# Attention in two layers: the exponentials of a unit issued one unit later than its scores and maxima

## The chip, the cores and the metric

The kernel runs on one core of a Trainium2 chip. Its time is the device time of one execution in microseconds (us). A core has TensorE (PE) for matrix products, VectorE (DVE), ScalarE (ACT) and GpSimd (POOL) for the rest, and SyncE (SP), which here only issues loads. Each engine takes its instructions in the order in which the program gives them. Matrix products write to PSUM, eight banks of 128 x 512 float32, and ACT and DVE read them from there.

## The reference, cut to what matters

Two layers over 256 latent and 256 context tokens. Each layer normalizes, projects, runs a pooling mixer and a differential attention side by side, projects out, and ends with a mixture of 32 experts. The attention, which the change concerns, is for each of four heads

```python
def diff_attend(q, k, v, lam):
    s = jnp.einsum('bqhmd,bkhmd->bhmqk', q, k).astype(jnp.float32) * (ATTN_HEAD_DIM ** -0.5)
    p = jax.nn.softmax(s, axis=-1)          # m = 0, 1: two maps a head
    a = p[:, :, 0] - lam * p[:, :, 1]
    return jnp.einsum('bhqk,bkhe->bqhe', a.astype(v.dtype), v)
```

Context queries see the 256 context keys, latent queries all 512 keys. In the second layer only latent queries are left.

## The kernel before, in words

A layer is `mixer`, which ends with the output projection, and `Moe`, which streams the experts' weights from memory. In `mixer` the attention works in *units*: one block of 128 queries and one head. Layer 0 has 16 units (the first 8 are context queries with 256 keys, the last 8 latent ones with 512), layer 1 has 8, all with 512 keys. A unit goes through four functions:

- `scores(i)`: PE makes two score tiles `S` (L712), DVE takes each row's maximum (L714) and scales it to the negative bias `nb` (L717), and ACT makes two exponentials `e` out of `S` with the row sums (L720). With that the two PSUM buffers of `S` come free.
- `probs(i)`: DVE turns the sums into a factor (L729, L730) and combines the two maps into one tile (L731).
- `turned(i)`: PE turns that tile (L739) into the PSUM tile `aT`, and ACT copies it to `t` (L741).
- `values(i)`: PE multiplies `t` with the values (L753) into `o`, and ACT squares the result for the norm (L755).

The code that stands around them sets each engine's order, word for word. `scores` of units 0, 1, 2 and `probs(0)` come first, mixed with pieces of the pooling mixer (`pool_a`: tile `pl`, copied at L686; `pool_b`: tile `pm`, copied at L694 and split at L463) and with broadcasts `bc` copied at L456. Then the loop runs over the units: `turned(i)`, `probs(i + 1)`, `scores(i + 3)`, `values(i)`, and other work behind it: pieces of the modulation (`ada`, L414), products of the output projection (`wo`, L467 to L469, twelve matrix products each), and the splitting of its weights `wout` into a high part `wh` (ACT) and a low part `wl` (DVE and POOL), both at L463 and L464, in runs of four pieces.

All PSUM tiles but one come from seven buffers, handed out in the order in which they came free. `e` has five buffers; from unit 2 to unit 6 of layer 0 two of them hold a bias of the modulation.

Of the kernel before, what the change touches and what calls it, by code (L numbers as in the profile page):

```python
# [231 lines left out]
def backbone_kernel(ctx: ExitStack, tc: tile.TileContext, x, par_d, lam_d, modb_d, adaw, win, wout, wx, rw_d, pw_d, fg_d,  # L232
# [16 lines left out]
    def w2(tag, dt=F32, shape=None):  # L249
        uid[0] += 1  # L250
        return work.tile(shape or [128, 512], dt, tag=tag, bufs=BUFS[tag], name=f"{tag}{uid[0]}")

    def small(shape, dt=F32, tag="sm", bufs=4):
        uid[0] += 1
        return work.tile(shape, dt, tag=tag, bufs=bufs, name=f"{tag}{uid[0]}")
# [10 lines left out]
    def pump():  # L266
        while pending and len(SB.slots) - pending[0][1] >= keep[pending[0][0][0] == "xf"] and (pending[0][0][0] != "xf" or early[0] > 0):
            key, n, fn = pending.popleft()
            early[0] -= key[0] == "xf"
            loaded[key] = fn()  # L270
# [17 lines left out]
    def fill(us):  # L288

        while us > 0.3 and fillers:  # L290
            key, t, fn = fillers[0]
            if key not in loaded:
                return
            fillers.popleft()
            fn()
            us -= t
# [256 lines left out]
    def mixer(l, W3, rows, pre, late=None):  # L553
# [122 lines left out]
        def pool_a(g):  # L676
            p = PS.get([128, 512], F32, "pl")

            for s in ((1,) if last else (0, 1)):
                for kt, cs in ((0, slice(0, 128)), (1, slice(112, 128)), (1, slice(128, 256)), (0, slice(128, 144))):  # L680
                    o = 256 * s
                    pe.matmul(p.t[:, o + cs.start:o + cs.stop], lhsT=u.t[:, 2 * s + kt, g * 128:g * 128 + 128],
                              rhs=band.t[:, (2 * g + kt) * 256 + cs.start:(2 * g + kt) * 256 + cs.stop],
                              start=kt == cs.start // 128, stop=kt != cs.start // 128)
            pT[g] = w2("m")
            act.activation(pT[g][:, c0:], p.t[:, c0:], AF.Copy)  # L686
            p.free()

        def pool_b(g):
            p = PS.get([128, 512], F32, "pm")  # L690
            pe.matmul(p.t[:, c0:], lhsT=pw[:, g], rhs=pT[g][:, c0:], start=True, stop=True)
            ps_ = par[:, P_PS + 4 * l + g:P_PS + 1 + 4 * l + g]
            m = w2("m")
            act.activation(m[:, c0:], p.t[:, c0:], AF.Copy, scale=ps_)  # L694
            p.free()
            split(m[:, c0:], cP[0][:, g], cP[1][:, g], gp)
# [3 lines left out]
        st, opsum, sums, sq, scaled = {}, {}, {}, {}, {}  # L700

        def scores(i):
            qt, h = units[i]
            nk = 512 if qt >= 2 else 256
            if h == 0:
                sums[qt] = small([128, 4, 2], tag="ls", bufs=3)
            mx, l_ = small([128, 2], tag="mx"), sums[qt][:, h]
            S, e = [], []
            for m in range(2):
                p = PS.get([128, 512], F32, "S")  # L710
                ms = slice(64 * m, 64 * m + 64)
                pe.matmul(p.t[:, :nk], lhsT=qT.t[ms, h, qt * 128:qt * 128 + 128], rhs=kT.t[ms, h, :nk],  # L712
                          start=True, stop=True)
                dve.reduce_max(mx[:, m:m + 1], p.t[:, :nk], axis=AX.X)  # L714
                S.append(p)
            nb = small([128, 2], tag="nb")
            dve.tensor_scalar(nb, mx, -0.125, None, op0=OP.mult)  # L717
            for m in range(2):
                e.append(w2("e"))
                act.activation(e[m][:, :nk], S[m].t[:, :nk], AF.Exp, scale=0.125, bias=nb[:, m:m + 1],  # L720
                               accum_out=l_[:, m:m + 1])
                S[m].free()
            st[i] = (e, l_, nk)

        def probs(i):

            e, l_, nk = st[i]
            r = small([128, 1], tag="rl")
            dve.reciprocal(r, l_[:, 1:2])  # L729
            stt(r, r, lamn[:, l:l + 1], l_[:, 0:1], op0=OP.mult, op1=OP.mult)  # L730
            stt(e[0][:, :nk], e[1][:, :nk], r, e[0][:, :nk], op0=OP.mult, op1=OP.add)  # L731
            st[i] = (e[0], nk)

        def turned(i):
            a, nk = st[i]
            n = nk // 128
            p = PS.get([128, 4, 128], F32, "aT")
            for kt in range(n):
                pe.transpose(p.t[:, kt], a[:, kt * 128:kt * 128 + 128], ident)  # L739
            aT = w2("t").rearrange("p (a b) -> p a b", a=4)  # L740
            act.activation(aT[:, :n], p.t[:, :n], AF.Copy)  # L741
            p.free()
            st[i] = (aT, n)
# [61 lines left out]
        def split_w(nb, kh):  # L805

            def part(k):
                if k == 0:
                    raw = need((key, nb, kh))
                    W[nb, kh] = SB.get([128, 4, 512], F32R, "wh"), SB.get([128, 4, 512], F32R, "wl"), raw  # L810
                hi, lo, raw = W[nb, kh]
                split(raw.t[:, k], hi.t[:, k], lo.t[:, k], dve if k % 2 else gp)
                if k == 0:
                    reserve()
                if k == 3:
                    W[nb, kh] = hi, lo
                    raw.free()
            return [(0.65, lambda k=k: part(k)) for k in range(4)]
# [34 lines left out]
        def pool_part():  # L853
            for nb in range(2):
                if nb and not (last and len(SPLITS) > 0):
                    steps.extend(split_w(1, 0))
                for t in qtiles:
                    steps.append((2.6, lambda t=t, nb=nb: out_unit(t, nb, 0)))
                steps.append((0, lambda nb=nb: release(W.pop((nb, 0)))))
            steps.append((0, lambda: release(pooled)))  # L860
            if not (last and len(SPLITS) > 1):
                steps.extend(split_w(0, 1))
            steps.append((0, lambda: moe or start_moe()))
            if not (last and len(SPLITS) > 2):
                steps.extend(split_w(1, 1))

        def release(hs):
            for h in hs:
                h.free()
# [70 lines left out]
        def start_moe():  # L940
            nonlocal moe
            rw = w2("o")[:, :320].rearrange("p (k n) -> p k n", k=8)
            act.dma_start(rw, rw_d[l].rearrange("p (k n) -> p k n", k=8))
            moe = Moe(l, qtiles, g1 if last else SB.get([128, 2, D], F32, "g2"), rw)
            moe.modulations()
            keep[1] = left[0]

        def spare():

            if moe and any(f[0][0] == "ada" and f[0] in loaded for f in fillers):  # L950
                fill_any()
            elif fillers and (fillers[0][0][0] == "bc" or len(fillers) > RES):
                fill(0.9)

        N = len(units)
        keep[:] = 0, 99
        scores(0)
        pool_a(0)
        for _, fn in split_w(0, 0):
            fn()  # L960
        fill(0.9)
        scores(1)
        pool_a(1)
        pool_b(0)
        fill(0.9)
        probs(0)
        scores(2)
        pool_a(2)
        pool_b(1)
        fill(0.9)  # L970
        for i in range(N):
            turned(i)
            if i + 1 < N:
                probs(i + 1)
            if i + 3 < N:
                scores(i + 3)
            if i == 0:
                pool_a(3)
                pool_b(2)
            if i == 1:  # L980
                pool_b(3)
                release((u, band))
                pool_part()
            if i == MOE_AT[l]:
                start_moe()
            if last and i in SPLITS:
                for _, fn in split_w(*((1, 0), (0, 1), (1, 1))[SPLITS.index(i)]):
                    fn()
            spare()
            values(i)  # L990
            while later and later[0][0] <= i:
                later.popleft()[1]()
            clock[0] += 3.0
            if i == N - EARLY_AT[l]:
                early[0] = EARLY[l]
                pump()
            if i > 1:
                proceed(STEP[l])
# [825 lines left out]
    for cb, k in order:  # L1824
        queue_ada(1, cb, [k])
    want_experts(0)
    moe = mixer(0, [], (ring, {}), pre)

    def next_loads():
# [33 lines left out]

    late = moe.run(next_loads, tail, at_end)
    moe = mixer(1, W3, (rs.pop(), dict(enumerate(rs))), {}, late)

    def finish():
# [51 lines left out]
```

## Time and profile before

| what | us |
|---|---|
| three runs | 961.01, 964.27, 965.11; median 964.27 |
| the profiled execution: its own time | 960.57 |
| its span, first to last instruction | 958.8 |
| PE busy | 814.8 (85%) |
| DVE busy | 441.7 (46%) |
| ACT busy | 265.8 (28%) |
| POOL busy | 174.1 (18%) |
| mean granted TensorE clock | 0.937 of full speed |
| memory read and written | 346 GB/s over the span |

The attention of layer 0 runs from about 148 to 256 us of the span, that of layer 1 from about 678 to 720 us. The shares are averages over stages with different limits: in the expert stages PE and the loads are busy nearly all the time, while in the attention four engines hand work to each other. So the trace is read by stage: which engine stands idle in the attention, and what ends that.

### The profile page before, as it was taken

What the parts mean: (1) busy time and instruction counts of PE and PEld (TensorE: products, weight loads), DVE (VectorE), ACT (ScalarE), POOL (GpSimd) and SP (SyncE); (2) the same over time, 40 slices, a digit from 0 to 9 for tenths busy, and PEclk for the clock granted to TensorE, in tenths of its full rate; (3) what the DMA queues carried; (4) which work ended last, traced back from release to release, by engine and by line L of the source; (5) the groups of instructions that cost most, each with busy time, mean ns of one, the idle gap of its engine ahead of it and who ended that gap; (6) DMA issues with size and microseconds to landing.
All of it is one profiled execution on the core that took longest, in us unless ns stands there. A gap on an engine that the chain in (4) does not pass through costs nothing.

```text
span 958.8 us, 13409 instructions
## 1 busy us (share of the span) xinstructions
PE 814.8 (85%) x4841; PEld 442.2 (46%) x4841; DVE 441.7 (46%) x965; ACT 265.8 (28%) x593; POOL 174.1 (18%) x192
## 2 busy tenths in 40 slices
PE   4799999988995879899976876899879679999973
PEld 1467765545784333333321224687557533443311
DVE  0533414566566222322211846654665735766633
ACT  1532216345441111111100015532572311111101
POOL 1400002233612101111101000000135211222212
PEclk9699999999997899999988997999999689999997
DMA  9989388830628999999999994672237589999992
GB/s 374 417 336 351 133 311 317 337 122 8 246 106 320 376 395 407 418 417 419 417 419 417 382 393 198 224 282 88 99 131 271 220 344 417 418 419 414 419 401 77
DMA packets 49081, 293.80 MB, mean 306 GB/s; under 512 B 7480, under 2 KB 7864, under 8 KB 16752
## 3 DMA queue, kind: packets, MB, share of 16 engines
q1 hardware_dynamic: 37008, 266.78, 69.3%
q0 software_dynamic: 6192, 13.84, 3.7%
q10 hardware_dynamic: 5808, 12.25, 3.4%
q8 instruction: 41, 0.67, 0.3%
q14 instruction: 32, 0.26, 0.1%
HBM read 317.29 MB, written 14.78 MB: 346 GB/s over the span
## 4 chain that ended last, share of the span: by engine, by line
PE 27%; DMA 26%; DVE 7%; ACT 2%; issue 1%; POOL 1%; SPq 0%; POOLq 0%; DVEq 0%; ACTq 0%
DMA we<-in_wx_dram 23%; PE gu L1447 8%; PE dn L1482 5%; DMA ada<-in_adaw_dram 2%; PE pj L599 2%; PE pj L467 2%; PE pj L468 2%; PE pj L469 2%; DMA h<-hd,ix 1%; DVE m L1514 1%; DVE o L1230 1%; PE rowps L414 1%; PE hTp L1268 1%; DVE X L1516 1%; PE hTp L1266 1%
## 5 line engine op out<-in xcount | busy, mean ns | idle before, releaser
L1482 PE MATMUL dn<-we,t 128*32 128x512 f32 (+2 forms) x672 | 108.2, 639 | 6.7 <-DMA we<-in_wx_dram 5.0
L1453 DVE SCALAR_TENSOR_TENSOR t<-t,tb,gu 128x256 f32<-128x256 f32 x25 | 12.0, 481 | 174.1 <-ACT t L1452 174.1
L1447 PE MATMUL gu<-we,hT0modl 128*32 128x512 f32 (+1 forms) x400 | 66.0, 631 | 10.8 <-DMA we<-in_wx_dram 10.1
L1452 ACT ACTIVATE t<-gu 128x256 f32<-128x256 f32 x25 | 9.6, 385 | 224.0 <-PE gu L1447 224.0
L1447 PE MATMUL gu<-we,hT0modh 128*32 128x512 f32 (+1 forms) x400 | 63.6, 628 | 7.1 <-DMA we<-in_wx_dram 6.3
L414 PE MATMUL rowps<-ada,sT 128*32 128x512 f32 x384 | 54.7, 658 | 13.7 <-DMA ada<-in_adaw_dram 13.7
L1482 PEld LDWEIGHTS dn<-we,t 128*32 128x32 f32 (+2 forms) x672 | 29.8, 121 | 66.8 <-issue 53.6
L467 PE MATMUL pj<-hH,wh 128*128 128x512 f32 (+1 forms) x128 | 47.6, 372 | 0.0
L1447 PE MATMUL gu<-we,hT1modl 128*32 128x512 f32 (+1 forms) x272 | 42.6, 604 | 5.5 <-DMA we<-in_wx_dram 5.5
L1516 POOL TENSOR_TENSOR X<-X,m 128x512 f32<-128x512 f32 x20 | 25.6, 1278 | 117.5 <-DVE m L1514 117.3
L469 PE MATMUL pj<-hH,wl 128*128 128x512 f32 (+1 forms) x128 | 46.4, 363 | 0.0
L468 PE MATMUL pj<-hL,wh 128*128 128x512 f32 (+1 forms) x128 | 46.4, 363 | 0.0
L1516 DVE TENSOR_TENSOR X<-X,m 128x512 f32<-128x512 f32 x36 | 43.5, 1208 | 1.3
L1447 PEld LDWEIGHTS gu<-we,hT0modl 128*32 128x32 f32 (+1 forms) x400 | 17.8, 121 | 54.7 <-issue 36.5
L1447 PE MATMUL gu<-we,hT1modh 128*32 128x512 f32 (+1 forms) x272 | 40.4, 625 | 2.5 <-DMA we<-in_wx_dram 1.4
L720 ACT ACTIVATE e<-S,nb 128x512 f32<-128x512 f32 (+1 forms) x48 | 29.2, 613 | 46.7 <-DVE nb L717 31.5
L1447 PEld LDWEIGHTS gu<-we,hT0modh 128*32 128x32 f32 (+1 forms) x400 | 16.9, 120 | 49.4 <-issue 36.5
L714 DVE TENSOR_REDUCE mx<-S 128x1 f32<-128x512 f32 (+1 forms) x48 | 26.8, 596 | 27.6 <-PE S L712 27.4
L1514 DVE TENSOR_TENSOR m<-cb,g 128x512 f32<-128x512 f32 x56 | 36.7, 682 | 0.1
L1249 POOL DMA_INDIRECT h<-hd,ix x14 | 14.4, 1027 | 123.3 <-DVE iy L1256 50.1
L753 PE MATMUL o<-v,t 128*128 128x128 f32 x160 | 24.5, 293 | 10.1 <-ACT t L741 10.1
L753 PEld LDWEIGHTS o<-v,t 128*128 128x128 f32 x160 | 20.1, 194 | 26.2 <-ACT t L741 23.6
(347 smaller groups left out, 1582.0 us busy)
## 6 DMA issues: line engine op xcount, KB each, us to landing
we<-in_wx_dram SPq DMA_DIRECT2D x207, 1024.0 KB
ada<-in_adaw_dram SPq DMA_DIRECT2D x48, 1024.0 KB
YD<-m ACTq DMA_DIRECT2D x1, 4096.0 KB
yb<-YD POOLq DMA_DIRECT2D x4, 1024.0 KB, 22.5
X<-in_x_dram SPq DMA_DIRECT2D x4, 512.0 KB
e<-in_modb_dram ACTq DMA_DIRECT2D x8, 256.0 KB
band<-in_band_dram SPq DMA_DIRECT2D x2, 1024.0 KB
hd<-h ACTq DMA_DIRECT2D x4, 512.0 KB
```

The costliest lines, as they stand in the source:

```text
L414: pe.matmul(rowps[l][32 * j:32 * j + 32], lhsT=sT[:, k, 4 - 2 * cb:36 - 2 * cb], rhs=h.t[:, 512 * j:512 * j + 512], start=cb < 2 and k == ...
L467: pe.matmul(ps, lhsT=lh, rhs=rh, start=first, stop=False)
L468: pe.matmul(ps, lhsT=lh, rhs=rl, start=False, stop=False)
L469: pe.matmul(ps, lhsT=ll, rhs=rh, start=False, stop=last)
L599: pe.matmul(p.t, lhsT=H[kh].t[:, k, ts], rhs=W3[kh][part].t[:, k], start=n == 0, stop=n == 23)
L714: dve.reduce_max(mx[:, m:m + 1], p.t[:, :nk], axis=AX.X)
L720: act.activation(e[m][:, :nk], S[m].t[:, :nk], AF.Exp, scale=0.125, bias=nb[:, m:m + 1], accum_out=l_[:, m:m + 1])
L753: pe.matmul(o.t[:, h], lhsT=aT[:, kt], rhs=v.t[:, kt, h * 128:h * 128 + 128], start=kt == 0, stop=kt == n - 1)
L1447: pe.matmul(p.t[r], lhsT=hT[k // 4][:, k % 4, r], rhs=gate_up(weights(w, k // 4), k), start=k == 0, stop=k == 7)
L1482: pe.matmul(ps[n2].t[r], lhsT=aT[:, k, r], rhs=down_w(weights(w, 2), k, n2), start=k == 0, stop=k == 1)
L1514: tt(m, q, self.g2[stream(t)][:, ns], op=OP.mult)
L1516: e.tensor_tensor(X[:, t, ns], X[:, t, ns], m, op=OP.add)
```

## The change

`scores` loses its last part, the two exponentials, which become a function `exps`. What `exps` needs, the two score tiles and `nb`, is kept until then. In the loop `exps(i + 2)` stands right behind `turned(i)`, ahead of `probs(i + 1)` and `scores(i + 3)`: the exponentials of a unit are given to ACT one pass of the loop after its scores. No instruction is added or removed on any engine, and nothing changes on POOL and SP but line numbers. Lines from L720 on move by 5, from the start of the loop by up to 9.

```diff
             mx, l_ = small([128, 2], tag="mx"), sums[qt][:, h]
-            S, e = [], []
+            S = []
             for m in range(2):
...
             dve.tensor_scalar(nb, mx, -0.125, None, op0=OP.mult)
+            st[i] = (S, nb, l_, nk)
+
+        def exps(i):
+            S, nb, l_, nk = st[i]
+            e = []
             for m in range(2):
                 e.append(w2("e"))
                 act.activation(e[m][:, :nk], S[m].t[:, :nk], AF.Exp, scale=0.125, bias=nb[:, m:m + 1],
...
         scores(1)
+        exps(0)
         pool_a(1)
         pool_b(0)
         fill(0.9)
+        scores(2)
+        exps(1)
         probs(0)
-        scores(2)
         pool_a(2)
         pool_b(1)
         fill(0.9)
         for i in range(N):
             turned(i)
+            if i + 2 < N:
+                exps(i + 2)
             if i + 1 < N:
                 probs(i + 1)
             if i + 3 < N:
```

On ACT in layer 0, from the copy of unit 11 on, the order before is as follows; `S_93` and `S_94` are the scores of unit 14, `aT_92` and `aT_95` the turned tiles of units 11 and 12, `wh` one of the weight splits.

```order
L741 ACTIVATE t153_1698<-aT_92_1693 128x512
L720 ACTIVATE e157_1713,ls136_1600<-S_93_1705,nb156_1711 128x512
L720 ACTIVATE e158_1715,ls136_1600<-S_94_1708,nb156_1711 128x512
L755 ACTIVATE t159_1721,rn130_1559<-o_81_1558 128x128
L463 ACTIVATE wh_87_1723<-('wout', 0)_75_1169 128x512 x4
L741 ACTIVATE t160_1738<-aT_95_1733 128x512
```

And now, at the same place, with `S_88` and `S_89`, the scores of unit 13:

```order
L746 ACTIVATE t151_1694<-aT_92_1689 128x512
L725 ACTIVATE e152_1696,ls136_1600<-S_88_1650,nb147_1656 128x512
L725 ACTIVATE e153_1698,ls136_1600<-S_89_1653,nb147_1656 128x512
L760 ACTIVATE t157_1717,rn128_1555<-o_81_1554 128x128
L463 ACTIVATE wh_87_1719<-('wout', 0)_75_1165 128x512 x4
L746 ACTIVATE t158_1734<-aT_95_1729 128x512
```

Between the two copies the kinds of instructions are the same, but the exponentials are those of the unit whose scores and maxima were issued one pass earlier.

On ACT at the start of layer 1's attention, before (`modh1` ends the modulation, `S_307` and `S_308` are unit 0, `S_312` and `S_313` unit 1):

```order
L436 ACTIVATE modh1_5529<-e392_5160 128x512
L720 ACT_TABLE_LOAD
L720 ACTIVATE e402_5551,ls399_5541<-S_307_5543,nb401_5549 128x512
L720 ACTIVATE e403_5553,ls399_5541<-S_308_5546,nb401_5549 128x512
L686 ACTIVATE m404_5560<-pl_309_5555 128x256
L463 ACTIVATE wh_183_5562<-('wout', 1)_166_5237 128x512 x4
L456 ACTIVATE g1_182_5540<-bc_310_5572 128x512
L456 ACTIVATE g1_182_5540<-bc_311_5576 128x512
L720 ACTIVATE e407_5589,ls399_5541<-S_312_5581,nb406_5587 128x512
L720 ACTIVATE e408_5591,ls399_5541<-S_313_5584,nb406_5587 128x512
L686 ACTIVATE m409_5598<-pl_314_5593 128x256
```

And now:

```order
L436 ACTIVATE modh1_5529<-e392_5160 128x512
L686 ACTIVATE m402_5556<-pl_309_5551 128x256
L463 ACTIVATE wh_183_5558<-('wout', 1)_166_5237 128x512 x4
L456 ACTIVATE g1_182_5540<-bc_310_5568 128x512
L456 ACTIVATE g1_182_5540<-bc_311_5572 128x512
L725 ACT_TABLE_LOAD
L725 ACTIVATE e405_5585,ls399_5541<-S_307_5543,nb401_5549 128x512
L725 ACTIVATE e406_5587,ls399_5541<-S_308_5546,nb401_5549 128x512
L686 ACTIVATE m407_5594<-pl_314_5589 128x256
```

The pool copy, the split and the two broadcast copies have moved ahead of unit 0's exponentials, and the table load has gone with the exponentials; the copy of unit 1's `pl` no longer stands behind unit 1's exponentials.

On ACT near the end of layer 1's attention, before: the copy of unit 5 (`aT_340`) and the last split that stands among the units.

```order
L755 ACTIVATE t458_5808,rn457_5803<-o_339_5802 128x128
L741 ACTIVATE t460_5822<-aT_340_5817 128x512
L463 ACTIVATE wh_185_5828<-('wout', 1)_173_5384 128x512 x4
L755 ACTIVATE t462_5842,rn457_5803<-o_339_5802 128x128
L741 ACTIVATE t464_5851<-aT_341_5846 128x512
```

And now:

```order
L760 ACTIVATE t456_5804,rn455_5799<-o_339_5798 128x128
L746 ACTIVATE t458_5818<-aT_340_5813 128x512
L725 ACTIVATE e459_5820,ls430_5692<-S_337_5790,nb454_5796 128x512
L725 ACTIVATE e460_5822,ls430_5692<-S_338_5793,nb454_5796 128x512
L463 ACTIVATE wh_185_5828<-('wout', 1)_173_5384 128x512 x4
L760 ACTIVATE t462_5842,rn455_5799<-o_339_5798 128x128
L746 ACTIVATE t464_5851<-aT_341_5846 128x512
```

The exponentials of the last unit, unit 7, now stand between that copy and the split.

## Rows read from the trace of the kernel before

**Rows 1.** The chain that ended last, in order of time: start, us, what.

```profile
406.95 20.57 DMA we<-in_wx_dram
...
697.67 1.28 DVE mx L714 x2
699.18 1.45 ACT e L720 x4
701.70 0.50 ACT t L741
702.24 1.16 PE o L753 x8
...
842.38 18.62 DMA we<-in_wx_dram
```

**Rows 2.** Waits from 146 to 250 us: total us, times, longest.

```profile
ACT e L720 <- DVE nb L717: 23.3, 11, 4.6
...
PE o L753 <- ACT t L741: 6.3, 4, 3.3
```

**Rows 3.** Timeline of PE, layer 0: start, us, what, [idle before <-releaser].

```profile
143.48 2.76 PE L414 MATMUL rowps<-ada,sT 128*32 128x512 f32 x24
...
193.54 1.79 PE L712 MATMUL S<-kT,qT 64*128 64x512 f32 x4 [0.33 <-ACT e L720]
...
203.32 0.71 PE L753 MATMUL o<-v,t 128*128 128x128 f32 x4 [1.42 <-ACT t L741]
...
207.49 2.35 PE L712 MATMUL S<-kT,qT 64*128 64x512 f32 x4
...
232.55 1.66 PE L753 MATMUL o<-v,t 128*128 128x128 f32 x8 [3.29 <-ACT t L741]
234.14 3.90 PE L414 MATMUL rowps<-ada,sT 128*32 128x512 f32 x24
...
240.90 1.16 PE L753 MATMUL o<-v,t 128*128 128x128 f32 x8 [1.27 <-ACT t L741]
```

**Rows 4.** Timeline of ACT, layer 0, units 11 to 13.

```profile
225.65 0.60 ACT L741 ACTIVATE t<-aT 128x512 f32<-128x512 f32 x1 [0.25 <-PE aT L739]
228.23 0.69 ACT L720 ACTIVATE e<-S,nb 128x512 f32<-128x512 f32 x1 [1.98 <-DVE nb L717]
...
229.82 2.19 ACT L463 ACTIVATE wh<-('wout', 0)_75_1169 128x512 fp32r<-128x512 f32 x4
...
236.58 0.69 ACT L720 ACTIVATE e<-S,nb 128x512 f32<-128x512 f32 x1 [4.08 <-DVE nb L717]
```

**Rows 5.** Timeline of PE, layer 1.

```profile
689.93 0.77 PE L691 MATMUL pm<-m,o 128*128 128x256 f32 x2 [2.57 <-ACT m L686]
690.49 1.06 PE L739 MATMUL aT<-cst,e 128*128 128x128 f32 x4
...
703.76 1.13 PE L712 MATMUL S<-kT,qT 64*128 64x512 f32 x4
...
706.44 1.13 PE L712 MATMUL S<-kT,qT 64*128 64x512 f32 x4
...
709.69 0.60 PE L739 MATMUL aT<-cst,e 128*128 128x128 f32 x4
```

**Rows 6.** Timeline of ACT, layer 1.

```profile
678.68 1.28 ACT L720 ACT_TABLE_LOAD   x1
...
682.51 2.19 ACT L463 ACTIVATE wh<-('wout', 1)_166_5237 128x512 fp32r<-128x512 f32 x4
...
711.20 2.20 ACT L463 ACTIVATE wh<-('wout', 1)_173_5384 128x512 fp32r<-128x512 f32 x4
```

**Rows 7.** Timeline of DVE, layer 1.

```profile
683.70 3.02 DVE L464 TENSOR_TENSOR wl<-('wout', 1)_166_5237,wh 128x512 fp32r<-128x512 f32 x2 [2.83 <-ACT wh L463]
```

**Rows 8.** Stretches of layer 0: length, busy us by engine, granted clock, DMA share, GB/s.

```profile
196.00:206.00 10.00, 6.95 (x42) 3.95 (x39) 5.59 (x10) 5.32 (x13) 4.65 (x3) 1.00 0.56 211
...
226.00:236.00 10.00, 6.71 (x40) 3.57 (x40) 6.38 (x10) 4.51 (x12) 4.92 (x4) 0.85 0.00 0
```

## The prediction

> **What bounds the kernel now.** I read the page's shares first, then the chain that ended last, then the waits and each engine's timeline within the two attention stretches. In the chain the long steps are loads of expert weights, 20.57 us from 406.95 and 18.62 us from 842.38 [rows 1]: the expert stages are held by the stream of weights. The attention is not: in 226 to 236 us the loads stand still (share 0.00), while PE is busy 6.71 us of 10, DVE 3.57, ACT 6.38 and POOL 4.51 [rows 8]. No engine is full there, so the time lies in waits for one another. In layer 1 the chain shows the ring that they form: maxima on DVE (L714, 1.28 for two), exponentials on ACT (L720, 1.45 for a pair), copy `t` on ACT (0.50), values on PE (L753, 1.16) [rows 1].
>
> The waits tell which link is late. ACT waits for `nb` in front of the exponentials 23.3 us in 11 waits, and PE waits for ACT's copy `t` 6.3 us in 4 [rows 2]. The two are one thing seen twice. ACT takes its instructions in order, and the exponentials of a unit stand ahead of the copy of an earlier unit. While ACT stands at exponentials whose maxima PE and DVE are only making, it can't copy, and PE stands at the values. Idle time of ACT alone would cost nothing; what counts is the 6.3 us on PE and PE's waits for score buffers.
>
> **Layer 0, buffers (A).** The scores at 193.54 wait 0.33 us and then take 1.79 instead of 1.13, those at 207.49 take 2.35 instead of 1.13 [rows 3, 5]: 0.33 + 0.66 + 1.22 = 2.2 us, in which the group stops for a buffer that earlier exponentials hold. With the exponentials a pass later these buffers are held longer, but all seven go round, so which release a score tile needs changes too. Following the rotation in the new order, I find scores that wait for a copy of the same pass (0.60, [rows 4], half of it hidden), twice, and once for a DVE step of about the same length: estimate 1.0 us. Net gain 1.2; bounds 0 and 2.2.
>
> **Layer 0, the copy of unit 12 (B).** Before the values at 232.55 PE is idle 3.29 us, released by `t` [rows 3]. On ACT the copy of unit 11 is over at 226.25, the next exponentials wait 1.98 us for `nb` until 228.23, and behind them come a square, four weight splits (2.19 us) and then the copy PE wants [rows 4]. Now the exponentials there have had their `nb` for a pass, so the 1.98 goes. The square still needs unit 11's values, and the splits still stand ahead of the copy. I take 1.7: the 1.98 less about half of a copy's 0.60. Bounds: 1.0 (half the wait, if the square comes late) and all 3.29.
>
> **Layer 0, the next copy (C).** Exponentials wait 4.08 us for `nb` until 236.58 [rows 4], and the values at 240.90 have 1.27 us of idle ahead [rows 3]. Without that wait the copy is done while PE runs 24 modulation products (3.90 us, [rows 3]): the 1.3 goes whole, covered by these products. Without that cover at most the same 1.3 would stay.
>
> **Layer 0, the clock (D).** Behind the idle 3.29 the values at 232.55 take 1.66 us against 1.16 at 240.90, and 24 products at 234.14 take 3.90 against 2.76 at 143.48 [rows 3]; the granted clock of this stretch is 0.85, a mix of the upper level with the lower [rows 8]. That is 0.50 + 1.14 = 1.6 us. After B the idle ahead of it is about 1.6. The nearest row is the idle of 1.42 at 203.32, in a stretch that kept a clock of 1.00 [rows 3, 8], so I take the whole 1.6; bounds 0 and 1.6. The 1.42 itself stays: there ACT is busy with splits and copies, not waiting at exponentials.
>
> Layer 0: 1.2 + 1.7 + 1.3 + 1.6 = 5.8 us.
>
> **Layer 1, the start (E).** Unit 0 is turned at 690.49, behind a `pm` product that waited 2.57 us for the copy of `pl`, which stood behind unit 1's exponentials [rows 5]. Two moves act here. The pool copy, the split and the broadcasts go ahead of unit 0's exponentials, and with them go 1.28 of table load and two exponentials of 0.69 [rows 6, 4], 2.66 together; since the copy of `pl` waits for its own product, the split comes about 2.1 earlier than 682.51 [rows 6]. DVE's two `wl` (3.02 us, having waited 2.83 for the split [rows 7]) come that much earlier, and then the maxima of units 1 and 2 (1.28 for two, [rows 1]). The exponentials of unit 0, and the table load directly before them, now lie on the path to `probs(0)`. The turn comes at about 688.5: gain 2.0. Bounds 0.7 (the load's 1.28 counts once more) and 2.6 (all of the wait).
>
> The Trainium skill, "ScalarE: Activation LUTs", section "What ACT_TABLE_LOAD costs", puts a drain of 1380 ns behind the 1283 ns of a load. The trace has the 1.28 [rows 6], and no row here shows a drain apart from it. By the page the gain of E would be 1.4 smaller, and the time 1.4 longer; the sum goes without it.
>
> **Layer 1, the loop (F).** From the turn of unit 0 at 690.49 to that of unit 5 at 709.69 it is 19.2 us, 3.84 a unit, while near its end two units' scores stand 706.44 - 703.76 = 2.68 apart [rows 5]. At 2.68 five units are 13.4 us; three pool pieces like the `pm` of 0.77 [rows 5] make it 15.7, a gain of 3.5. Each unit has four maxima and `probs` on DVE and a pair of exponentials on ACT, which keep some of it; I take 3.0. Bounds: 1.5 (a pair of exponentials, 1.45 [rows 1], leaves the ring once) and 19.2 - 13.4 = 5.8.
>
> **Layer 1, the end (G).** The exponentials of unit 7 now stand ahead of the last four splits at 711.20 [rows 6] and of the copies behind them: a loss of 1.45 at most [rows 1], which I take; the other bound is 0.
>
> Layer 1: 2.0 + 3.0 - 1.45 = 3.6. The rest of the change (the list `e`, the tuple that is kept) makes no instruction, and POOL and SP are moved past nothing.
>
> **What becomes of the gain.** The loads stand still in the attention [rows 8] because their buffers are full, and they start again when the expert stage takes the buffers. So a shorter attention starts that stream earlier, and I carry the gain over whole: 5.8 + 3.6 = 9.4 us. The profiled execution has 960.57 us, 3.7 below the median of 964.27; it would come to 951.2. The same gain off the median gives 964.27 - 9.4 = **954.9 us**. The least by the bounds above is 0 + 1.0 + 1.3 + 0 + 0.7 + 1.5 - 1.45 = 3.05, or 961.2; the most 2.2 + 3.3 + 1.3 + 1.6 + 2.6 + 5.8 = 16.8, or 947.5.
>
> **Rivals.** *Layer 1 keeps its pace.* Four maxima, `probs`, exponentials and copies may set the loop's 3.84 by themselves, so that F is 0, and E gives its least. The stretch of 2.68 speaks against it, the ring in the chain for it, since there the exponentials start 0.23 us after the maxima end [rows 5, 1]. Gain 5.8 + 0.7 - 1.45 = 5.05: 959.2 us.
>
> *The stream hides it.* If the loads of 20.57 and 18.62 us [rows 1] don't start earlier, the end stays where it is: 964.3 us. The load share of 0.00 speaks against it [rows 8], as such a queue waits for the program and not for memory.
>
> *Slower by the clock.* In the new order the scores of a unit hold two buffers a pass longer, so fewer of the seven are left for everything else, and PE may stop shortly and often where it now stops seldom and long. If the clock then falls to its lower level in the latent units, PE's work there takes 3.90 / 2.76 = 1.41 times as long [rows 3]. From 193.54 to 240.90 and from 690.49 to 709.69 there are 66.6 us [rows 3, 5]; at a PE share as in 226 to 236 (0.67, [rows 8]) that is 45 us of work, 18 us more, and 18 - 9.4 = 9 us slower: 973 us. It outweighs the gain from 23 us of PE work at the lower level. Against it: the stretch 196 to 206 has stops of both kinds, PE at 6.95 of 10 and a clock of 1.00 [rows 8].
>
> The Trainium skill names such a course in "TensorE: Matmul & The Clock Gate", section "A second HAM failure mode: psum-queue depth-cycling": PE idles briefly between groups as its PSUM banks go round, and the clock swings between its levels. The clock of 1.00 in a stretch with two stopped score groups does not bear it out.
>
> That the change doesn't do what it says I rule out by the order: the exponentials do stand a pass later on ACT.
>
> **How the numbers follow.** The forecast has a chance of 0.68, layer 1 keeping its pace 0.17, the hidden gain 0.08, the clock 0.07. A difference of 0.5%, 4.8 us, is about what a measurement of this kernel can tell from none, so faster means below 959.4. Of the forecast's 0.68 all but 0.05 lies below it, and of the first rival half: 0.63 + 0.09 = 0.72. Within 0.5%: 0.05 + 0.08 and most of the hidden case, 0.20. Slower: the clock, and the rest, 0.08. The range from 947.5 to 961.5 takes in the bounds of the sum and the first rival, and leaves out the other two and a little of the tails.
>
> **What would show it.** ACT's 23.3 us of waits for `nb` fall to a few, and PE's 6.3 us for `t` to about 3 (B, C). The idle ahead of the two value groups that stand around the 24 modulation products near 230 us is near 1.6 and near 0, and those products take 2.8 (D). Score groups of unequal length remain, shorter ones (A). In layer 1 unit 0 is turned about 2 us sooner after the modulation, the table load stands directly before unit 0's exponentials (E), the five units take some 16 us (F), and the last splits start behind unit 7's exponentials (G). I am wrong if the copy is late all the same, since splits and squares stand before it, if score groups stop longer than 2 us, if the granted clock of the latent units falls below what it is, or if both attentions shorten and the span doesn't.

## The result, and the profile after

The changed kernel took 950.13 us in the median of four executions (948.50 to 953.53), the kernel before 962.64 (957.66 to 965.11): a ratio of 0.9891 on record, with an interval of 0.9859 to 0.9923 (the quotient of these two medians alone is 0.9870, inside it). It was measured once more with the later experiments, in twelve executions: 953.3 us (946.92 to 960.14) beside 961.22, a ratio of 0.9933 (0.9908 to 0.9958). The two intervals share 0.9908 to 0.9923, so the change is worth some 8 us of 961 if both hold, and single executions of the changed kernel spread by 13 us. Both facts are taken up below. The prediction was 954.9 after 964.27, which is 0.9903.

The profiled executions have spans of 958.8 and 946.7 us, 12.1 apart. To see where these lie, take three rows of PE from each trace: the transposes of the shift that stand ahead of each layer's first scores (`shp`), and the first output product behind layer 1's attention (`wo`). Columns are start, us, what, [idle before <-releaser]. Before:

```profile
147.84 0.66 PE L441 MATMUL shp<-cst,e 128*128 128x128 f32 x4 [1.60 <-DVE e L433]
...
677.35 0.60 PE L441 MATMUL shp<-cst,e 128*128 128x128 f32 x4
...
720.11 0.48 PE L467 MATMUL wo<-wh,cp 128*128 128x512 f32 x1
```

After:

```profile
147.08 0.66 PE L441 MATMUL shp<-cst,e 128*128 128x128 f32 x4 [1.60 <-DVE e L433]
...
670.13 0.60 PE L441 MATMUL shp<-cst,e 128*128 128x128 f32 x4
...
708.40 0.47 PE L467 MATMUL wo<-wh,cp 128*128 128x512 f32 x1
```

0.76 us were won ahead of the first attention, where the change does nothing; that is chance. From one `shp` to the other it is 529.51 and 523.05 us (6.46 less), from the second `shp` to `wo` 42.76 and 38.27 (4.49 less), from `wo` to the end 238.7 and 238.3. So nearly all of the gain lies in the two attentions, and what is won there is still there at the end.

In layer 0 the rows of PE that answer to [rows 3] are these:

```profile
185.04 1.73 PE L712 MATMUL S<-kT,qT 64*128 64x512 f32 x4
...
205.06 2.13 PE L712 MATMUL S<-kT,qT 64*128 64x512 f32 x4
...
211.42 1.94 PE L712 MATMUL S<-kT,qT 64*128 64x512 f32 x4
...
228.59 1.16 PE L758 MATMUL o<-v,t 128*128 128x128 f32 x8 [1.52 <-ACT t L746]
229.68 2.78 PE L414 MATMUL rowps<-ada,sT 128*32 128x512 f32 x24
...
234.40 1.16 PE L758 MATMUL o<-v,t 128*128 128x128 f32 x8 [0.35 <-ACT t L746]
```

The idle time ahead of unit 12's values has gone from 3.29 to 1.52 us, that of unit 13 from 1.27 to 0.35, and the 24 modulation products take 2.78 in place of 3.90. Of the waits from 146 to 250 us (total us, times, longest), ACT's for `nb`, 23.3 us in [rows 2], has left the list. ACT now waits for the turned tile itself, which is what it is there for, and PE's wait for the copy has halved:

```profile
ACT t L746 <- PE aT L744: 23.9, 10, 2.8
...
PE o L758 <- ACT t L746: 3.3, 3, 1.5
```

The granted clock, 1.00 at the upper of its two levels and 0.50 at the lower, has risen at three places. These are stretches (length; busy us of PE, PEld, DVE, ACT, POOL; clock; load share; GB/s) of before:

```profile
256.00:266.00 10.00, 9.72 (x69) 8.51 (x68) 3.16 (x6) 3.94 (x10) 8.37 (x12) 0.89 0.94 372
...
690.00:710.00 20.00, 17.52 (x97) 11.19 (x98) 14.32 (x38) 15.11 (x46) 3.11 (x5) 0.91 0.32 121
```

And of after, the first one being that of [rows 8]:

```profile
226.00:236.00 10.00, 8.13 (x60) 3.98 (x60) 8.47 (x18) 8.54 (x22) 5.64 (x6) 1.00 0.06 16
...
256.00:266.00 10.00, 9.72 (x62) 8.32 (x58) 7.12 (x21) 3.48 (x7) 3.35 (x5) 1.00 0.62 256
...
690.00:710.00 20.00, 16.02 (x113) 11.64 (x110) 14.31 (x33) 14.96 (x42) 6.77 (x9) 1.00 0.37 140
```

In layer 1, on PE, units 0 and 5 are turned at 682.18 and 696.89; the rows answer to [rows 5]:

```profile
678.40 1.12 PE L712 MATMUL S<-kT,qT 64*128 64x512 f32 x2 [0.61 <-ACT e L725]
...
682.18 0.63 PE L744 MATMUL aT<-cst,e 128*128 128x128 f32 x4 [1.14 <-DVE rl L734]
...
694.30 0.60 PE L744 MATMUL aT<-cst,e 128*128 128x128 f32 x4
...
696.89 0.60 PE L744 MATMUL aT<-cst,e 128*128 128x128 f32 x4
...
702.39 1.16 PE L758 MATMUL o<-v,t 128*128 128x128 f32 x8 [1.61 <-ACT t L746]
```

Units 4 and 5 are 2.59 us apart, and PE stands idle nowhere between them. The start and the end of this attention still have idle time, ahead of unit 0's turn (1.14) and of unit 6's values (1.61).

### The profile page after: what moved, and what is told of

Same layout as the page of the kernel before. It is cut to its first block, busy times and chain, and to the rows that moved or that the text cites. A ratio compares the mean times of both kernels' runs of the same rounds, so it can differ in the third digit from the quotient of the medians.

```text
span 946.7 us, 13424 instructions
## 1 busy us (share of the span) xinstructions
PE 804.3 (85%) x4841; PEld 438.4 (46%) x4841; DVE 441.7 (47%) x965; ACT 267.0 (28%) x593; POOL 175.1 (18%) x192
## 4 chain that ended last, share of the span: by engine, by line
PE 33%; DMA 19%; DVE 8%; ACT 2%; issue 1%; POOL 1%; POOLq 0%; SPq 0%; DVEq 0%; ACTq 0%
DMA we<-in_wx_dram 16%; PE gu L1456 12%; PE dn L1491 6%; PE pj L599 2%; DMA ada<-in_adaw_dram 2%; PE pj L467 2%; PE pj L468 2%; PE pj L469 2%; DVE o L1239 1%; DVE m L1523 1%; DMA h<-hd,ix 1%; PE hTp L1277 1%; PE rowps L414 1%; DVE X L1525 1%; PE S L712 1%
## 5 line engine op out<-in xcount | busy, mean ns | idle before, releaser
L1491 PE MATMUL dn<-we,t 128*32 128x512 f32 (+2 forms) x672 | 103.3, 615 | 6.2 <-DMA we<-in_wx_dram 4.5
L1491 PEld LDWEIGHTS dn<-we,t 128*32 128x32 f32 (+2 forms) x672 | 27.6, 118 | 63.8 <-issue 52.4
L467 PEld LDWEIGHTS pj<-hH,wh 128*128 128x128 f32 x128 | 24.1, 188 | 11.9 <-issue 8.4
```

The costliest lines, as they stand in the source:

```text
L467: pe.matmul(ps, lhsT=lh, rhs=rh, start=first, stop=False)
L1491: pe.matmul(ps[n2].t[r], lhsT=aT[:, k, r], rhs=down_w(weights(w, 2), k, n2), start=k == 0, stop=k == 1)
```

## The experiments

In each experiment three distances are read from the trace: from `shp` to `shp` (layer 0 and its experts), from `shp` to unit 0's and unit 5's turn in layer 1, and from `shp` to `wo` there. They don't depend on where an execution began.

| kernel | shp to shp | turn of unit 0, unit 5 | shp to wo | ratio to before, interval |
|---|---|---|---|---|
| before | 529.51 | 13.14, 32.34 | 42.76 | |
| changed, first profile | 523.05 | 12.05, 26.76 | 38.27 | 0.9891, 0.9859 to 0.9923 |
| changed, second profile | 522.43 | 12.05, 26.76 | 38.27 | 0.9933, 0.9908 to 0.9958 |
| layer 0 only | 522.86 | 13.59, 32.58 | 43.13 | 0.9934, 0.9910 to 0.9957 |
| layer 1 only | 528.70 | 12.04, 28.87 | 40.39 | 0.9969, 0.9949 to 0.9990 |
| loop only | 525.56 | 13.22, 29.38 | 41.85 | 0.9940, 0.9922 to 0.9958 |
| start only | 529.53 | 12.05, 29.71 | 40.27 | 0.9972, 0.9953 to 0.9992 |
| longer stop in layer 0 | 529.23 | 12.06, 26.76 | 40.27 | 0.9963, 0.9942 to 0.9985 |
| exponentials ahead of the copy | 535.41 | 12.06, 31.73 | 42.98 | 0.9964, 0.9942 to 0.9986 |
| table loaded early | 522.07 | 11.24, 25.94 | 38.41 | 0.9890, 0.9854 to 0.9926 |
| last exponentials later | 522.05 | 12.05, 30.47 | 40.65 | 0.9884, 0.9835 to 0.9932 |
| both of these | 522.21 | 11.23, 25.94 | 36.13 | 0.9899, 0.9861 to 0.9938 |
| both, and low parts on POOL | 525.44 | 10.65, 25.35 | 35.54 | 0.9866, 0.9835 to 0.9896 |

**One layer alone.** With the kernel before's calls for the other layer:

```diff
             st[i] = (S, nb, l_, nk)
+            if last:            # layer 1 as before; "not last" in the other kernel
+                exps(i)
...
-            if i + 2 < N:
+            if i + 2 < N and not last:
                 exps(i + 2)
```

> The later exponentials in layer 0 only; layer 1 as before. Theory (ACT's copies are no longer late, and each layer keeps its gain to the end): the two traces give 5.7 us in the attention of layer 0, and 0.7 of it more at the better clock behind, so about -6.4 us, a ratio of 0.993; the attention of layer 1 takes its old time, unit 0 to unit 5 turned in 19.2 us. Rival (the stream of weights takes the gain of the first layer back, and only what is gained in the last layer counts): 0 us.

> The later exponentials in layer 1 only; layer 0 as before. Theory: -4.5 us, a ratio of 0.995, unit 0 to unit 5 turned in 14.7 us as in the changed kernel. Rival (the granted clock of layer 1, 0.91 before and 1.00 after in 20 us of it, is what gained, and it comes from layer 0): the clock stays at 0.91 and the five units take 16 us or more, -2.5 us or less.

Layer 0 alone gave 0.9934, some 6.3 us as the theory had it, and the whole of it lies ahead of the second `shp` (6.65 in the trace). The stream of weights hides nothing: from `wo` to the end it is 238.7 us in this kernel (951.1 - 669.27 - 43.13), as before. Layer 1 alone gave 0.9969, 3.0 us with an interval of 1 to 5; the theory's 4.5 is inside, the rival's 2.5 too, so the time doesn't decide between them. In its trace units 0 and 5 are turned 16.83 us apart, not 14.7, since the clock fell in the first of them (stretch of that kernel):

```profile
685.00:690.00 5.00, 4.80 (x14) 2.37 (x14) 2.87 (x8) 4.30 (x12) 1.46 (x2) 0.50 0.24 100
```

That the clock of 1.00 comes from layer 0 does not follow from it: the kernel with the last exponentials moved has the change in layer 0 too, and its clock fell at the same place (below).

**Start or loop.** The exponentials of units 0 to 2 where they were and only later ones delayed (loop), or those of units 0 and 1 delayed, unit 2's behind `probs(0)`, and all later ones at once (start):

```diff
+            if i < 3:           # start only: i > 2
+                exps(i)
...
-            if i + 2 < N:
+            if i + 2 < N and i + 2 > 2:     # start only: False
                 exps(i + 2)
```

> Units 0 to 2 of each layer have their exponentials where they were before; from unit 3 on they come a pass later. Theory: the start was worth 0.9 us in layer 0 and 1.1 in layer 1, the loop the rest, so -8 to -10 us, a ratio of 0.990 to 0.992; unit 0 of layer 1 is turned as late as before, 13.1 us after the first scores. Rival (the new order of the start did it, since probabilities of unit 0 no longer stand ahead of unit 2's maxima): -2 us.

> The reverse: the exponentials of units 0 and 1 come one unit later, with the new order of the start, and from unit 2 on they follow their scores at once, as before. Theory: -2 us, a ratio of 0.998; the idle time of 3.3 us ahead of the values of unit 12 in layer 0, and the slower modulation products behind it (3.9 us), come back. Rival (the start did it): -8 us.

Loop 0.9940 and start 0.9972, 5.8 and 2.7 us: the loop is the larger part, though with less than the 8 to 10 expected, and the two add up to 8.5, about the whole. The traces are clear on layer 0. Values and modulation products at unit 12 with the start only, where all is as before but for a clock still lower:

```profile
230.10 1.16 PE L760 MATMUL o<-v,t 128*128 128x128 f32 x8 [3.29 <-ACT t L748]
231.19 4.48 PE L414 MATMUL rowps<-ada,sT 128*32 128x512 f32 x24
...
238.45 1.16 PE L760 MATMUL o<-v,t 128*128 128x128 f32 x8 [1.20 <-ACT t L748]
```

And with the loop only:

```profile
228.38 1.16 PE L760 MATMUL o<-v,t 128*128 128x128 f32 x8 [1.52 <-ACT t L748]
229.47 2.78 PE L414 MATMUL rowps<-ada,sT 128*32 128x512 f32 x24
...
234.18 1.05 PE L760 MATMUL o<-v,t 128*128 128x128 f32 x7 [0.35 <-ACT t L748]
```

So the idle time and the clock at unit 12 go with the delayed exponentials of the loop. Layer 1's first turn goes with the start (12.05 with it, 13.14 to 13.59 without).

Two distances repeat so closely from profile to profile that they settle the matter better than the times. From `shp` to the values of unit 13 in layer 0 it is 87.25 to 87.32 us in all seven profiles with the whole change there and nothing added, 88.47 with the loop only, 92.13 with the start only and 93.06 before: 4.6 us go with the loop and 0.9 with the start. From the turn of unit 1 to that of unit 5 in layer 1 it is 13.73 us before, with layer 0 only and with the start only, and 10.77 in the changed kernel, with layer 1 only and with the loop only: 2.96 us go with the loop. What does not repeat is the way from unit 13 to the second `shp`, 434.6 to 438.1 us in the thirteen profiles, kernels with and without the change mixed; so the 0.7 us that the changed kernel's first profile won there can't be put down to the change.

**A longer stop.** To see whether the clock at unit 12 hangs on the idle time, the copy of unit 12 was done five times in place of once, on the same tile:

```diff
+            if l == 0 and i == 12:
+                for _ in range(4):
+                    act.activation(aT[:, :n], p.t[:, :n], AF.Copy)
             act.activation(aT[:, :n], p.t[:, :n], AF.Copy)
```

> The changed kernel with the copy of unit 12 in layer 0 done four times more on ACT (same tile, same data), some 2 us of added work ahead of the values that now wait 1.5 us, so that their idle time is 3.5 as it was 3.3 before the change. Theory (the longer stop is what lowers the granted clock there): the values take 1.7 and the 24 modulation products behind them 3.9 or more, and the values of unit 13 come 3.6 us later than in the changed kernel. Rival (the clock fell for another reason): the products take 2.8, and only the 2.0 us are lost.

```profile
230.88 1.16 PE L761 MATMUL o<-v,t 128*128 128x128 f32 x8 [4.04 <-ACT t L749]
231.97 4.44 PE L414 MATMUL rowps<-ada,sT 128*32 128x512 f32 x24
...
238.34 1.16 PE L761 MATMUL o<-v,t 128*128 128x128 f32 x8 [0.36 <-ACT t L749]
```

The stop grew by 2.52 us, half a microsecond more than meant, and the products behind it went from 2.78 to 4.44: 1.66 us on top of the work added. From the values of unit 12 to those of unit 13 it is 7.46 us, against 5.81. Those of unit 13 come 5.25 us later than in the changed kernel, not 3.6: 2.52 and 1.66 of it are these two, and 1.08 had been lost earlier, in a stretch with a clock of 0.97 (147 to 200 us). The clock at this place hangs on the stop ahead of it. The kernels agree: in all eight profiles with a stop of 1.52 the products take 2.78; behind a stop of 2.86 (the next kernel) they take 3.64, behind 3.29 in three kernels 3.90, 4.48 and 4.55, and behind 4.04 4.44.

**Ahead of the copy.** The exponentials are as late as in the changed kernel, but stand before the copy of the same pass on ACT:

```diff
         for i in range(N):
-            turned(i)
             if i + 2 < N:
                 exps(i + 2)
+            turned(i)
```

> The changed kernel with the exponentials of unit i + 2 ahead of the copy of unit i on ACT, where they stand behind it; TensorE's order is the same. Theory (what counts is when the copy is done): the copy comes 1.4 us later in each unit, which PE's score products (1.1 us) cover only in part. Layer 1: 0.9 to 1.3 us more for each of five units, so 17 to 19 us from unit 0's turn to unit 5's in place of 14.7, and one or two us in layer 0: ratio to before 0.995 to 0.998. Rival (only the wait for the maxima counted, and that is gone here too): 0.989 as in the changed kernel.

0.9964, in the range of the theory. But the loss is larger than it had: where the clock was at the upper level, nothing of the loop's gain is left. From the turn of unit 1 to that of unit 5 in layer 1 it is 13.88 us, against 10.77 in the changed kernel and 13.73 before. In layer 0 it is 14.27 us from the values of unit 11 to those of unit 13, against 9.99 and 14.30, though the clock fell behind unit 12 here, as it did before. ACT no longer waits for `nb`; it waits in front of the square for the values, and the values wait for the copy (ACT's row, then two of PE):

```profile
710.16 0.28 ACT L760 ACTIVATE t<-o 128x128 bf16<-128x128 f32 x1 [1.31 <-PE o L758]
```

```profile
708.91 1.16 PE L758 MATMUL o<-v,t 128*128 128x128 f32 x8 [0.85 <-ACT t L746]
...
712.41 1.16 PE L758 MATMUL o<-v,t 128*128 128x128 f32 x8 [0.85 <-ACT t L746]
```

So a new ring of about 3.5 us a unit has formed: copy, values, square, exponentials, next copy. In the loop, ACT's order here differs from that of the kernel before only in that the square, and pool copies and splits where there are any, stand ahead of the exponentials and not behind them. Without the place behind the copy the late issue is worth nothing in either loop. What remains, 0.36%, is about what the start alone gave (0.28%), and the start is as in the changed kernel (unit 0 turned at 12.06).

Five units took 19.67 us, over the 17 to 19 expected, since the first of them took 5.79 at a lower clock (0.83 in 690 to 710 us). The 535 us from `shp` to `shp` are not the edit's alone: in this execution, the slowest of its twelve, the clock was about 0.5 from 152 to 162 us, which cost 6.3 us up to unit 0's values, at instructions that stand there in the changed kernel too.

**The table, and the last exponentials.** An exponential of one column right behind layer 1's first scores brings the table load forward. The second kernel gives out the last unit's exponentials one pass later, behind the last splits; the third does both.

```diff
         scores(0)
+        if last:
+            act.activation(small([128, 1], tag="rl"), ident[:, 0:1], AF.Exp)
...
-            if i + 2 < N:
+            if i + 2 < N and not (last and i + 2 == N - 1):
                 exps(i + 2)
+            if last and i == N - 2:
+                exps(N - 1)
```

> The changed kernel with one more exponential, of one column, on ACT in layer 1 right behind the first scores, so that the table is loaded there and not in front of unit 0's exponentials. Theory (the table load of 1.28 us now lies on the way to the first probabilities, and DVE takes over behind it): unit 0 is turned 11.1 to 11.3 us after the shift's transposes (12.05 in the changed kernel), and the first output product of the layer comes 0.8 to 0.9 us earlier, at 37.4; time 0.999. Rival (DVE's splits and maxima set the start by themselves): no difference. If a load cost twice its row, as the page on activation tables has it, 1.3 to 2.7.

> The changed kernel, but the exponentials of layer 1's last unit stand one pass later, behind the splits and the copy of unit 6, where they stood ahead of them. Theory: the values of unit 6 no longer wait 1.6 us, and the loss at the end of layer 1 (1.3 us against the kernel before) comes back: first output product at 36.9 after the transposes, not 38.27. Rival (the last unit's probabilities are then late, and its turn sets the end): 38.3 or later.

> The changed kernel with both edits that were tried one by one: the table loaded early in layer 1, and the last unit's exponentials behind the last splits. Theory: 0.8 and 1.3 us in the trace, which add up unless the clock falls: unit 0 of layer 1 turned 11.2 us after the transposes, first output product at 36.1 (38.3 in the changed kernel); 0.987. Rival (the end of layer 1 waits for the router's and unit 7's work by now): not under 37.5.

On ACT in the changed kernel the load stands between the broadcast's copies and unit 0's exponentials, and costs its own 1.28 and no more (the copies end at 676.25, the exponentials begin at 677.57):

```profile
675.18 1.07 ACT L456 ACTIVATE g<-bc 128x512 f32<-128x512 f32 x2
676.27 1.28 ACT L725 ACT_TABLE_LOAD   x1
677.57 0.69 ACT L725 ACTIVATE e<-S,nb 128x512 f32<-128x512 f32 x1
```

With the load at 669.44, in ACT's idle time, the exponentials follow the copies, and unit 0 is turned 0.81 us earlier, as expected; DVE is what releases it:

```profile
669.44 1.28 ACT L964 ACT_TABLE_LOAD   x1
670.73 0.20 ACT L964 ACTIVATE rl<-cst 128x1 f32<-128x1 f32 x1
...
673.18 1.07 ACT L456 ACTIVATE g<-bc 128x512 f32<-128x512 f32 x2
674.14 0.69 ACT L725 ACTIVATE e<-S,nb 128x512 f32<-128x512 f32 x1
```

At `wo` the 0.81 was lost again, to products at a lower clock near the end of this execution's attention (the turn of unit 7 took 1.12 us, not 0.66), so the time shows nothing. With the last exponentials moved, unit 6's values wait 0.26 us, not 1.61, and from unit 5's turn to `wo` it is 10.18 us, not 11.51: 1.33 back, where 1.3 were expected:

```profile
702.65 1.16 PE L758 MATMUL o<-v,t 128*128 128x128 f32 x8 [0.26 <-ACT t L746]
```

But its ratio of 0.9884 can't be told from the changed kernel's either, and `wo` came at 40.65, where 36.9 was expected. The 3.7 between lie ahead of unit 5's turn, for in its profile the first units of layer 1 ran at the lower level (the same stretch of this kernel, and of the changed one's second profile):

```profile
680.00:685.00 5.00, 4.93 (x17) 3.13 (x18) 2.71 (x7) 2.83 (x7) 0.72 (x1) 0.50 0.01 3
```

```profile
680.00:685.00 5.00, 4.76 (x32) 3.64 (x34) 3.63 (x10) 4.23 (x13) 1.58 (x2) 1.00 0.19 41
```

Up to there the two kernels have the same instructions. From the first turn to the second it took 7.45 us in the one and 3.94 in the other. So the 3.5 us hang on the execution. Both edits together bring `wo` to 36.13, as the expectation had it (36.1), but their ratio of 0.9899 can't be told from the changed kernel's 0.9933 beside it, with such a scatter.

**Low parts on POOL.** In addition all four low parts of the first split in layer 1 go to POOL:

```diff
-                split(raw.t[:, k], hi.t[:, k], lo.t[:, k], dve if k % 2 else gp)
+                split(raw.t[:, k], hi.t[:, k], lo.t[:, k], dve if k % 2 and not (last and (nb, kh) == (0, 0)) else gp)
```

> The changed kernel once more, beside the two below. Theory: 0.989 as before, since the start and the loop together gave it. In layer 1's first two units the granted clock was 1.00 in its first profile and about 0.5 in 5 us of two kernels with the very same start (the one with the change in layer 1 alone, and the one with the last exponentials moved); if that changes by the execution and not by the kernel, single times spread by 3 us and more, and the shortest lie near 947.

> As table_lastexp, and in the start of layer 1 all four low parts of the weight split are made by POOL, none by DVE (two of four before, 3.0 us on DVE ahead of unit 1's maxima). Theory (behind the table load, these two DVE instructions hold the start, which is where the missing 0.9 us of the start's gain went): unit 0 is turned about 10.0 us after the transposes, first output product at 34.9; 0.986. Rival (the score buffers and ACT's order hold it): 11.2 as without.

The changed kernel's second measurement spreads as that expectation had it, from 946.92 to 960.14, but its ratio is 0.9933, not 0.989. In the last kernel unit 0 is turned at 10.65, half-way to the 10.0 expected. DVE has idle time now, and waits for scores:

```profile
676.98 1.29 DVE L714 TENSOR_REDUCE mx<-S 128x1 f32<-128x512 f32 x2 [1.25 <-PE S L712]
...
679.87 1.29 DVE L714 TENSOR_REDUCE mx<-S 128x1 f32<-128x512 f32 x2 [1.39 <-PE S L712]
```

So both the theory and its rival hold a part: DVE's two splits kept about 0.6 us, and behind them the scores of unit 2 wait for ACT's broadcast copies `g`, which stand behind the four splits (the group then takes 1.50 instead of 1.13 us, and what that 0.37 waits for is not named):

```profile
678.70 0.68 PEld L712 LDWEIGHTS S<-kT,qT 64*128 64x128 f32 x4 [0.33 <-ACT g L456]
```

Its ratio is the lowest of all, 0.9866 (0.9835 to 0.9896) with a median of 948.27 us, and its interval lies below that of the changed kernel measured beside it, 0.9933 (0.9908 to 0.9958). It is not below that of the changed kernel's first measurement (0.9859 to 0.9923).

## Why the prediction was right, step by step

The mechanism held: the maxima no longer hold up the copy, each layer gains for itself, and the gain reaches the end. Term by term, in the profiled executions:

| step | predicted | measured | from |
|---|---|---|---|
| A, score buffers in layer 0 | 1.2 | 0.5 | distance from `shp` to the values of unit 11: 78.76 and 77.33, less the start below |
| start of layer 0 | none | 0.9 | distance to the first values: 18.75 and 17.84 |
| B, copy of unit 12 | 1.7 | 1.8 | idle 3.29 and 1.52 |
| C, next copy | 1.3 | 0.9 | idle 1.27 and 0.35 |
| D, clock at unit 12 | 1.6 | 1.6 | 1.66 + 3.90 and 1.16 + 2.78 |
| layer 0 | 5.8 | 5.7 | |
| E, first turn in layer 1 | 2.0 | 1.1 | 13.14 and 12.05 |
| F, five units in layer 1 | 3.0 | 4.5 | 19.20 and 14.71; 1.5 of it the clock at unit 0 |
| G, end of layer 1 | -1.45 | -1.1 | from unit 5's turn to `wo`: 10.42 and 11.51 |
| layer 1 | 3.6 | 4.5 | |

**A** had the right waits and too small a price. The score groups at 185.04, 205.06 and 211.42 wait for the steps foreseen, a copy of the same pass twice and a DVE step once. Of PE's weight loads in the changed kernel:

```profile
185.65 0.29 PEld L712 LDWEIGHTS S<-kT,qT 64*128 64x128 f32 x2 [0.31 <-ACT t L746]
...
206.06 0.29 PEld L712 LDWEIGHTS S<-kT,qT 64*128 64x128 f32 x2 [0.71 <-DVE m L843]
...
212.23 0.29 PEld L712 LDWEIGHTS S<-kT,qT 64*128 64x128 f32 x2 [0.52 <-ACT t L746]
```

The three groups together take 0.60 + 1.00 + 0.81 = 2.4 us more than free ones of 1.13, not the 1.0 assumed. And before, one more group had stopped than the 2.2 of the sum counted:

```profile
186.74 1.85 PE L712 MATMUL S<-kT,qT 64*128 64x512 f32 x4
```

With its 0.72 it is 2.9 before, and 2.9 - 2.4 = 0.5. **The start** of layer 0 was not in the sum at all: before, unit 2's scores stopped for a buffer that earlier exponentials held, and PE went on 1.55 us after their start (156.37 to 157.92); now it goes on after 0.63. The two misses nearly cancel.

**B and D** came out as worked. The longer stop shows the link between them: give the idle time back, and the clock falls again. **C** was meant to go whole; 0.35 us stayed, as the copy comes that much after the products that cover it. The sum took only the exponentials' wait away; but the copy also stands behind four splits, and these start late, 1.46 us after ACT was free:

```profile
231.67 2.20 ACT L463 ACTIVATE wh<-('wout', 0)_78_1210 128x512 fp32r<-128x512 f32 x4 [1.46 <-PE rowps L414]
```

**E** was over-sized. Of 2.0 us 1.1 came. The split and DVE's low parts do start 2.2 earlier after `shp`, as worked; the rest of the path ate half of that. The working let DVE's splits and the table load run out ahead of unit 0 and left the rest to the maxima; the trace shows the load between the copies and the exponentials, the second half of unit 2's scores waiting 0.61 us for these, and DVE's maxima for the scores. The load early gives 0.8 back, the low parts on POOL 0.6. The Trainium skill, "ScalarE: Activation LUTs", section "What ACT_TABLE_LOAD costs", would have the load cost another 1380 ns of drain, and by an estimate from that figure the gain of E would be 1.4 smaller. The trace does not show that: the copies end 0.02 us before the load starts, and the exponentials start 0.02 us after its end.

**F** was right for the order, and what it brought beyond that is the clock. At the pace of 2.59 the loop is PE's, as the row of 2.68 had promised. From the turn of unit 1 to that of unit 5, at the upper level in both kernels, it is 13.73 us before (from 695.96) and 10.77 after (from 686.12): 2.96, where 3.0 were forecast. The other 1.53 lie between the first two turns, 5.47 before and 3.94 after. There the turn of unit 0, the scores and the pool products took 1.06, 2.08 and 1.22 us before, in a stretch of 0.91, and 0.63, 1.13 and 1.07 after:

```profile
691.48 2.08 PE L712 MATMUL S<-kT,qT 64*128 64x512 f32 x4
...
695.96 0.60 PE L739 MATMUL aT<-cst,e 128*128 128x128 f32 x4
```

```profile
682.74 1.13 PE L712 MATMUL S<-kT,qT 64*128 64x512 f32 x4
...
686.12 0.60 PE L744 MATMUL aT<-cst,e 128*128 128x128 f32 x4
```

The forecast had no term for this clock, so the 4.5 owe a third to something that it did not see.

**The rivals.** That layer 1 keeps its pace is refuted by 10.77 us for four units in place of 13.73, that the stream hides the gain by the layers tried alone and by the 238 us from `wo` to the end in nearly all kernels. The clock rival was wrong as a verdict and right as a danger. Its mechanism, PE stopping for buffers, did not lower the clock where it was looked for: in the changed kernel the stretch 200 to 226 has two of the stopped score groups and a clock of 1.00.

```profile
200.00:226.00 26.00, 25.07 (x126) 17.37 (x126) 20.56 (x40) 12.99 (x40) 11.03 (x10) 1.00 0.01 2
```

The prediction's own witness against it was misread: the stretch 196 to 206 has stops of 1.60 and 1.42 us, but the stopped score groups at 193.54 and 207.49 lie outside it; the clock was 1.00 there too (147 to 200 and 200 to 226 us of before). At the start of layer 1 the clock fell in some executions and not in others, with the same instructions and a loss of up to 3.5 us: of ten profiles with the new start there, three of them with the table loaded early, it fell in three (first to second turn 5.79, 6.06 and 7.45 us in place of 3.94). In the three with the start of before it fell each time (5.26 to 5.47). Whether the old start makes it fall, three profiles don't show. It adds to the spread of 947 to 960 us; how much of that, and of the difference between the two measurements, is open.

The sum of 9.4 us stands between the two measurements of about 10.5 and 6.4 (0.9891 and 0.9933 of 961). In the pair of profiles the attentions are 10.2 us shorter, 8.7 without the clock at layer 1's first units. Between the layers the changed kernel's profile won 0.7 more, with a clock of 1.00 in 256 to 266 us for one of 0.89, which is inside the scatter of that stretch; the rest of the 12.1 isn't traced to the change. That the sum came so near is in part luck: A, C and E fell short by 2.0 together, and the start of layer 0, the clock in F and the smaller loss at the end (G) made up 2.8 that were not in it.

## What to carry to other kernels

Where an engine takes its work in order, look at what stands behind a waiting instruction, not at the wait itself: ACT's 23 us of waits were worth 5.7 in layer 0, and these were two late copies, the clock behind one of them, and a few score buffers, some of them at the start. An instruction that must wait for a chain over other engines is best given out a pass later, behind the work that somebody waits for now; late but ahead of the copy, it brought the loops nothing. What a move brings to the start and the end of a loop needs its own working, as there the moved work meets loads, splits and tables that the loop does not have.

## What the runs showed of the hardware

A stop of PE has a price beyond itself at unit 12: with 1.52 us ahead, 24 products took 2.78 us in eight profiles, with 2.86 us 3.64, with 3.29 us 3.90, 4.48 and 4.55 in three kernels, with 4.04 us 4.44. Yet the same instructions ran at either level at the start of layer 1 (0.50 and 1.00 over 5 us, 3.5 us apart), so idle time in the order alone does not tell the level there; what does is open. Score groups that stopped 0.6 to 1.0 us for their buffers left the clock at 1.00. A table load in ACT's idle time delayed nothing that was seen; one between two busy stretches held ACT 1.28 us, of which 0.81 showed at the first turn.
